# Hybrid attention and RG-LRU layer on one core: projections as three f16 products with ranges found on the chip, instead of three float32r products

## The chip, the cores and the metric

The kernel runs on one NeuronCore of one Trainium2 chip. The metric is device time in microseconds, the median of several executions. For the kernel before it is 510.38 us (three runs, 509.89 to 511.35).

## What is computed

One layer over 1024 tokens with 16 meta tokens ahead of them (T = 1040), model width 1024:

```python
u = rms_norm(h, norm_w, EPS)            # h: meta tokens, then x
proj = u @ w_in                         # 1024 -> 3072
q, k, v, g_att, x_lru, g_lru = split(proj)            # 512 columns each
o = diff_attention(rope(q), rope(k), v, lam, chunk_ids)   # 4 heads, 2 maps each
att_out = rms_norm(o, subln_w) * (1 - lam_init) * silu(g_att)
xc = causal_conv(x_lru, conv_w, width 4) + conv_b
lru_out = rg_lru(xc, w_r, b_r, w_i, b_i, lru_L) * silu(g_lru)
h = h + concat([att_out, lru_out]) @ w_out
out = rms_norm(h, final_norm_w)[16:]
```

All inputs and the output are float32.

## The kernel before

The program is written out in order: each engine carries out its instructions in the order in which the Python code emits them, and nothing reorders them later. A small model of the engines' times (class Clock) only decides where waiting work (lists `bg`, `chains`, `fill`) is emitted between products.

A float32 product is made of three: both operands are split into a hi part and a lo part, and hi*hi, lo*hi and hi*lo are added up in PSUM (`fm_step`, `tm_step`). In the kernel before both parts are float32r. The contraction over 1024 is cut into eight chunks of 128 (k), and the weights come in six groups of 512 columns, in this order:

- **x_lru** (called XL here, L283 to L430). `head_start(k)` loads the k-th chunk of the weights and of x transposed, ScalarE makes the hi part (for x times norm_w), VectorE the lo part, and the products of three of the four channel blocks follow at once, chunk by chunk. The fourth block's products come behind. The row scale 1/rms of each token (`rstd`) is found beside this from a second copy of x (`load_xt`), and is written to DRAM and read back to all partitions (`Rb`); results of the projections are multiplied by it afterwards.
- **k, q, g_att, g_lru** (`run_group`): 32 steps of products each. While one group's products run, the next group's weights are fetched, split by `split_steps` (ScalarE hi, VectorE lo) and kept. Beside k, q and g_att the LRU's convolution, gates (products named psg) and scan are carried out from the list `bg`. k's products take all 1040 tokens in three column pieces (264, 264, 512), the others 512 columns at a time.
- **v, attention and output projection** (`attend`): the score, softmax and weighting steps of eight token tiles, with the products of v and of the output projection (`out_lru`, `out_att`) filled in between. w_out is loaded late by `load_wo`: ScalarE makes the hi part, GpSimd the lo part.

The scales that bring q, k and v into the range of f16 come from the sums of squares of norm_w times the weights (`f16_scale`).

Of the kernel before, what the change touches and what calls it, by code (L numbers as in the profile page):

```python
# [37 lines left out]
class Clock:  # L38
    """Rough times of the engines while the program is written, to place products that can wait
    where TensorE would otherwise stand."""  # L40
# [52 lines left out]
def hybrid_layer_kernel(ctx: ExitStack, tc: tile.TileContext, xT, x, meta, w6, nwT,  # L93
# [56 lines left out]
    def tick(us):  # L150
# [7 lines left out]
        while bg and bg[0][0] <= credit[0]:  # L158
# [4 lines left out]
            if f is None:       # the rest waits for the next chunk of products  # L163
                break
# [10 lines left out]
    CH = 1.25                    # one chunk of six float32r products  # L175

# [1 line left out]
    nw = cst([P, KC], name="nw")  # L178
    nc.gpsimd.dma_start(nw, nwT)
    xs, wt = {}, {}  # L180
    f2 = {g: cst([P, KC], name=f"f2_{g}") for g in (G_Q, G_K, G_V)}
    ss = cst([P, NT + 1], name="ss")
    V.memset(ss, 1.0)
    A.activation(ss, ss, AF.Copy)       # the activation table comes in beside the first loads
# [164 lines left out]
    for t in nxt:  # L349
        load_xt(t)  # L350
# [959 lines left out]
```

## Time and profile before

| | |
|---|---|
| runs | 509.89, 510.38, 511.35 us, median 510.38 |
| profiled execution, first to last instruction | 509.1 us; its whole time isn't listed, the median of the runs is 1.3 us above the span |
| TensorE busy | 473.1 us (93%), 2838 matmuls; weight loads 380.3 us (75%) |
| VectorE busy | 384.1 us (75%), 692 instructions |
| ScalarE busy | 296.8 us (58%), 549 instructions |
| GpSimd busy | 132.7 us (26%), 174 instructions |
| mean granted TensorE clock | 0.976 of full speed |

In the profile's rows PE is TensorE, PEld its weight loads, DVE VectorE, ACT ScalarE, POOL GpSimd, SP the queue that issues most DMAs. A group's row ends with the busy time in us and the mean ns of one instruction, then the idle time of the engine ahead of it. A timeline row has start and length in us, then the instruction, how many were merged, and in brackets the idle time ahead of it with what ended it. A row by windows has the stretch, its length, and the busy time (and number of instructions) of PE, PEld, DVE, ACT and POOL, then the granted clock, the DMA share and GB/s. A busy PE row counts matmuls that overlap one another or wait for weights; so products are measured here by the distance of their starts.

### The profile page before, as it was taken

How to read it: one execution, taken by the hardware profiler on the slowest of the kernel's cores; microseconds unless marked ns; L12 is line 12 of the kernel's file. 1: busy time of each engine (PE TensorE's matmuls, PEld its weight loads, DVE VectorE, ACT ScalarE, POOL GpSimd, SP SyncE). 2: the span in 40 equal slices, each digit the busy share in tenths (PEclk: the TensorE clock that was granted, in tenths of full speed). 3: DMA queues.
4: the chain of work that ended last, by engine and by line, in shares of the span. 5: the costliest groups of instructions: out<-in, count | busy, mean ns of one | idle time of the engine just before them, and what ended most of it. 6: DMA issues, size and time to landing. Idle time of an engine off the chain costs nothing.

```text
span 509.1 us, 7805 instructions
## 1 busy us (share of the span) xinstructions
PE 473.1 (93%) x2838; PEld 380.3 (75%) x2838; DVE 384.1 (75%) x692; ACT 296.8 (58%) x549; POOL 132.7 (26%) x174
## 2 busy tenths in 40 slices
PE   6999939999999999999999999787998899989994
PEld 5998839888888888888876667565776677867774
DVE  5664786693898676974674776899899999999643
ACT  5883532655436838423662466586686776676743
POOL 0110913100110000000100232157142415245772
PEclk9999969999999999999999999999799999989998
DMA  8971801145033114269551126584554374504433
GB/s 255 397 281 41 320 21 38 28 108 163 5 79 82 44 41 166 82 194 304 168 188 37 42 84 169 174 216 145 131 139 121 88 187 125 167 1 163 163 131 124
DMA packets 51366, 68.87 MB, mean 135 GB/s; under 512 B 22096, under 2 KB 31216, under 8 KB 51328
## 3 DMA queue, kind: packets, MB, share of 16 engines
q1 hardware_dynamic: 39456, 55.75, 33.7%
q0 software_dynamic: 11872, 12.63, 10.3%
q8 instruction: 22, 0.36, 0.3%
q14 instruction: 16, 0.13, 0.1%
HBM read 49.44 MB, written 18.91 MB: 134 GB/s over the span
## 4 chain that ended last, share of the span: by engine, by line
PE 56%; DVE 26%; DMA 6%; issue 5%; ACT 4%; POOL 2%; SPq 0%; POOLq 0%; DVEq 0%; ACTq 0%
PE pss L71 34%; DVE e L71 9%; DVE w L71 5%; DVE mx L71 5%; PE psv L71 5%; PE psoa L71 4%; PE psx L71 4%; PE ps L71 3%; PE psg L71 2%; DVE xres L71 2%; DMA r_d<-rstd 1%; PE O L71 1%; DMA Rb<-r_d 1%; DMA idf<-in_ident_dram 1%; ACT sq L71 1%
## 5 line engine op out<-in xcount | busy, mean ns | idle before, releaser
L71 PE MATMUL pss<-xs,w 128*128 128x512 f32 (+1 forms) x720 | 143.5, 347 | 4.7 <-ACT xs L71 4.2
L71 PEld LDWEIGHTS pss<-xs,w 128*128 128x128 f32 x720 | 121.5, 192 | 25.3 <-ACT xs L71 4.2
L71 ACT ACTIVATE e<-e,mx,esc 128x528 f32<-128x528 f32 (+7 forms) x64 | 56.4, 881 | 59.9 <-DVE mx L71 49.6
L71 DVE CUSTOM_DVE_ANT_0 e<-pss,mask 128x528 f32<-128x528 f32 (+7 forms) x64 | 49.0, 766 | 8.9 <-PE pss L71 8.9
L71 DVE TENSOR_TENSOR w<-wraw,w 128x512 fp32r<-128x512 f32 (+2 forms) x49 | 37.4, 780 | 20.6 <-ACT w L71 20.5
L71 PE MATMUL psv<-w,xs 128*128 128x512 f32 x192 | 48.7, 403 | 0.8 <-DVE v L71 0.8
L71 PE MATMUL psol<-woh,lr 128*128 128x512 f32 x128 | 42.7, 414 | 6.1 <-DVE v L71 2.7
L71 PE MATMUL pss<-w,xs 128*128 128x512 f32 x192 | 45.9, 394 | 0.0
L71 PE MATMUL pss<-kst,qt 128*128 128x512 f16 (+3 forms) x208 | 43.8, 324 | 0.6 <-DVE mx L71 0.6
L71 PE MATMUL psoa<-woh,at 128*128 128x512 f32 (+1 forms) x136 | 43.0, 399 | 1.1 <-ACT psoa L71 1.1
L71 PEld LDWEIGHTS psv<-w,xs 128*128 128x128 f32 x192 | 35.3, 188 | 10.6 <-DVE v L71 1.2
L71 PEld LDWEIGHTS pss<-w,xs 128*128 128x128 f32 x192 | 35.7, 188 | 7.9
L71 ACT COPY wT<-pt 128x1024 f16<-128x1024 f16 (+5 forms) x48 | 37.7, 784 | 0.9 <-PE pt L71 0.8
L71 ACT ACTIVATE w<-wraw 128x512 fp32r<-128x512 f32 x47 | 28.5, 619 | 12.8 <-DMA wraw<-in_w_dram 12.3
L71 PE MATMUL ps<-xs,w 128*128 128x512 f32 x120 | 35.0, 400 | 0.0
L71 PEld LDWEIGHTS psol<-woh,lr 128*128 128x128 f32 x128 | 22.9, 188 | 13.5 <-DVE v L71 3.2
L71 PEld LDWEIGHTS <-wT 128*128 128x128 f16 x432 | 27.1, 101 | 7.8 <-issue 5.0
L71 PE MATMUL O<-v,wT 128*128 128x128 f16 x432 | 30.6, 224 | 2.3 <-ACT o L71 2.3
L71 DVE SCALAR_TENSOR_TENSOR e<-e,mx 128x528 f32<-128x528 f32 (+7 forms) x32 | 29.6, 924 | 1.1
L71 POOL COPY wm<-w 128x32 f16<-128x32 f16 x32 | 7.6, 236 | 85.3 <-DVE w L71 84.0
L71 PE MATMUL pt<-idh,w 128*128 128x128 f16 x288 | 25.0, 225 | 5.1 <-ACT wT L71 3.5
L71 PEld LDWEIGHTS psoa<-woh,at 128*128 128x128 f32 x136 | 24.7, 195 | 6.3 <-ACT psoa L71 2.1
(190 smaller groups left out, 874.6 us busy)
## 6 DMA issues: line engine op xcount, KB each, us to landing
wraw<-in_w_dram SPq DMA_DIRECT2D x47, 256.0 KB, 4.2
xt<-in_x_dram SPq DMA_DIRECT2D x8, 512.0 KB, 6.8
woraw<-in_w_out_dram SPq DMA_DIRECT2D x8, 512.0 KB, 4.0
xres<-in_x_dram SPq DMA_DIRECT2D x8, 512.0 KB, 4.5
lr<-lru_d POOLq DMA_DIRECT2D x8, 512.0 KB, 5.1
res_d<-xres SPq DMA_DIRECT2D x8, 512.0 KB, 3.0
res<-res_d SPq DMA_DIRECT2D x8, 512.0 KB, 4.3
out_dram<-res SPq DMA_DIRECT2D x7, 512.0 KB, 2.9
```

The source lines that it names most:

```text
L71: return f(*a, **k)
```

## The change

The hi and lo parts of x, of the projections' weights, of the LRU output and of the attention output, and of w_out, become f16. For their range:

- Each weight group is scaled by the inverse of its whole norm, found on the chip: `square_w` takes squares and their sums on ScalarE, `norm_of` adds them over partitions by a product with ones and takes the power on GpSimd. The split (`split_steps`, now for two chunks of k at a time, 1024 columns) applies the scale. `load_wo` does the same for w_out, and its lo part moves from GpSimd to VectorE.
- x is normed before its split. It is loaded in four pieces of 260 tokens (p = 0 to 3) with all 1024 channels. `square_x` and `sum_x` find the row scales of a piece on the chip: squares on ScalarE, adds on VectorE, small products, a power on GpSimd, a product that spreads the row over all partitions. `split_x` then takes three steps for each of the eight chunks k: VectorE multiplies by norm_w and the row scale, ScalarE casts to hi, VectorE subtracts for lo.
- XL is now done piece by piece: for each p all eight `split_x`, then the products of blocks 0 and 1 (`xl_pair(p, 0)`, 48 products of 260 columns), then those of blocks 2 and 3 in two halves of 24, with `sum_x` of the next piece between the halves. Results are copied out by ScalarE. The weights of the other groups are fetched in two DMAs at the start of a group instead of eight.
- The multiplications by `Rb` and `rstd` after the projections go away, constants take their place, and the LRU output gets a scale per channel (one more pass of squares).

```diff
-    def load_x(k, cuts):
...
-        for c in cuts:
-            hi, lo = xa(0, k, c), xa(1, k, c)
-            A.activation(hi, raw[:, c], AF.Copy, scale=nw[:, k:k + 1])
-            V.scalar_tensor_tensor(lo, raw[:, c], nw[:, k:k + 1], hi.bitcast(F32), op0=OP.mult, op1=OP.subtract)
+    def sum_x(p, s):
+
+        for q in s:
+            V.tensor_tensor(q[:, 0:2], q[:, 0:2], q[:, 2:4], op=OP.add)
+        V.tensor_tensor(s[0][:, 0:2], s[0][:, 0:2], s[1][:, 0:2], op=OP.add)
+        a = s[0]
+        V.tensor_tensor(a[:, 0], a[:, 0], a[:, 1], op=OP.add)
+        ps = bank([XQ, 4], name="psx1")
+        for j in range(4):
+            PE.matmul(ps[:, j:j + 1], a[:, 0, j * XQ:(j + 1) * XQ], ones[:, 0:1], start=True, stop=True)
+        r = const.tile([XQ, 4], F32, tag="rst", bufs=2, name="rst")
+        V.tensor_scalar(r, ps, 2.0 ** -20 / D, EPS * 2.0 ** -20, op0=OP.mult, op1=OP.add)
+        G.tensor_tensor(r, r, pw[0:XQ, 0:4], op=OP.pow)
...
+        PE.matmul(pr_, ones[0:XQ, :], a[0:XQ, 2], start=True, stop=True)
+        return pr_
+
+    def split_x(p, rs, k):
+        s = slice(p * XP, (p + 1) * XP)
+        t = xraw[p, k // 4][:, k % 4]
+        if xs[k] is None:
+            xs[k] = slot("X", [P, 2, T], F16, name="xs")
+        V.scalar_tensor_tensor(t, t, nws[:, k:k + 1], rs, op0=OP.mult, op1=OP.mult)
+        A.activation(xs[k][:, 0, s], t, AF.Copy)
+        V.tensor_tensor(xs[k][:, 1, s], t, xs[k][:, 0, s], op=OP.subtract)
...
+    for p in range(4):
+        ps = two_banks()
+        for c in range(4):
+            if p == 0:
+                split_xl(0, c)
+            for k in (2 * c, 2 * c + 1):
+                split_x(p, rs, k)
+        if p == 0:
+            square_xl(1)
+            lam_steps()
+            for c in range(4):
+                split_xl(1, c)
+        if p < 3:
+            sq = square_x(p + 1)
...
+        xl_pair(p, 0, range(KC), ps)
+        xl_evac(p, 0, ps)
+        ps = two_banks()
+        xl_pair(p, 1, range(4), ps)
+        if p < 3:
+            rs = sum_x(p + 1, sq)
+        xl_pair(p, 1, range(4, KC), ps)
+        xl_evac(p, 1, ps)
+        if p == 1:
+            for h in range(2):
+                square_w(G_K, h)
+            norm_of(G_K, n2w[G_K])
+        if p == 2:
+            for k in range(0, KC, 2):
+                for _ in split_steps(G_K, k):
+                    pass
+            softplus_steps()
+            for h in range(2):
+                conv_scale(h)
...
+        for b, k in enumerate(ks):
+            r, s = raw[b // 2][:, b % 2], v[:, b:b + 1] if j else v[:, 0:1]
+            A.activation(wo[k][:, 0], r, AF.Copy, scale=s)
             yield
+            V.scalar_tensor_tensor(wo[k][:, 1], r, s, wo[k][:, 0], op0=OP.mult, op1=OP.subtract)
             yield
-            G.tensor_tensor(l, r, h.bitcast(F32), op=OP.subtract)
...
-            V.tensor_tensor(r[:, s], r[:, s], ps, op=OP.add)
+            V.scalar_tensor_tensor(r[:, s], ps, woc[0], r[:, s], op0=OP.mult, op1=OP.add)
```

The change's order stands first on ScalarE in the XL stage. Before, hi parts of weights (w) and of x (xs) alternate with squares of x (xt), and each waits for a DMA alone:

```order
L71 ACTIVATE w<-wraw 128x512 [waits DMAHW7_49]
L71 ACTIVATE xs<-xraw,nw 128x528 [waits DMAHW0_49]
L71 ACTIVATE xs<-xraw,nw 128x512 [waits DMAHW1_49]
L71 ACTIVATE xt,ss<-xt 128x1024 [waits DMAHW2_49,Activation_49]
L71 ACTIVATE w<-wraw 128x512 [waits DMAHW3_49]
```

Now, over pieces p = 1 and p = 2, the copies of the products' results (XL) and, ahead of p = 2, the squares of k's weights stand between the hi parts of one piece and of the next:

```order
L71 ACTIVATE xs<-xraw 128x260 [waits DVE_49] x8
L71 ACTIVATE xsq<-xraw 128x1040 [waits DMAHW0_49]
L71 ACTIVATE xsq<-xraw 128x1040 [waits DMAHW1_49]
L71 COPY XL<-pss 128x260 [waits PE_49]
L71 COPY XL<-pss 128x260
L71 COPY XL<-pss 128x260 [waits PE_49]
L71 COPY XL<-pss 128x260
L71 ACTIVATE w,n_3_521<-wraw 128x2048 [waits DMAHW4_49]
L71 ACTIVATE w,n_3_521<-wraw 128x2048 [waits DMAHW5_49]
L71 ACTIVATE xs<-xraw 128x260 [waits DVE_49] x8
```

The hi parts have moved from behind a DMA to behind VectorE's step of the same chunk, and behind the copy of the last products of the piece before.

On VectorE before, each x instruction makes a lo part and waits for its hi part:

```order
L71 SCALAR_TENSOR_TENSOR xs<-xraw,nw,xs 128x528 [waits DMAHW6_49,Activation_49]
L71 SCALAR_TENSOR_TENSOR xs<-xraw,nw,xs 128x512 [waits DMAHW7_49,Activation_49]
L71 TENSOR_TENSOR w<-wraw,w 128x512 [waits DMAHW4_49,Activation_49]
L71 SCALAR_TENSOR_TENSOR xs<-xraw,nw,xs 128x528 [waits DMAHW5_49,Activation_49]
L71 SCALAR_TENSOR_TENSOR xs<-xraw,nw,xs 128x512 [waits DMAHW6_49,Activation_49]
```

Now, in piece p = 0 (wsx is the weights' scale, psx the row scales in PSUM, nws norm_w):

```order
L71 SCALAR_TENSOR_TENSOR w<-wraw,wsx_158,w 128x2x256 [waits DMAHW2_49,Activation_49]
L71 SCALAR_TENSOR_TENSOR xraw<-xraw,nws,psx_149 128x260 [waits DMAHW0_49]
L71 TENSOR_TENSOR xs<-xraw,xs 128x260 [waits Activation_49]
L71 SCALAR_TENSOR_TENSOR xraw<-xraw,nws,psx_149 128x260
L71 TENSOR_TENSOR xs<-xraw,xs 128x260 [waits Activation_49]
L71 SCALAR_TENSOR_TENSOR w<-wraw,wsx_158,w 128x2x256 [waits Activation_49]
```

Each subtraction waits for ScalarE's cast of the product that VectorE wrote directly ahead of it, and the next chunk's multiplication stands behind the subtraction.

On TensorE, the first products wait behind the norm of the second half of the XL weights (n2x_214):

```order
L71 MATMUL psx_149<-xsq,ones 128x260 [waits DVE_49]
L71 MATMUL psf<-n2x_152,ones 128x1 [waits Activation_49]
L71 MATMUL psf<-n2x_214,ones 128x1 [waits PE_49,Activation_49]
L71 LDWEIGHTS w
L71 MATMUL pss<-xs,w 128x260
```

In the kernel before, the first product stands at the head of TensorE's order, with no product ahead of it. The small products of `sum_x` (psx) stand in the same way in the middle of each later pair, as the diff shows.

More of the change, by code (lines that the diff above doesn't have):

```diff
@@ L179, in hybrid_layer_kernel @@
     nc.gpsimd.dma_start(nw, nwT)
[L180 to L184, printed above, removed]
+    idf = cst([P, P], name="idf")
+    nc.gpsimd.dma_start(idf, ident)
+    idh = cst([P, P], F16, name="idh")
+    ones = cst([P, P], name="ones")
+    V.memset(ones, 1.0)
+    pw = cst([P, 16], name="pw")
+    V.memset(pw, -0.5)
+    two = cst([P, 16], name="two")
+    V.memset(two, 2.0)
+    e16 = cst([P, 1], name="e16")
+    V.memset(e16, 2.0 ** -116)
+    mone = cst([P, 1], name="mone")
+    V.memset(mone, -1.0)
+    A.activation(e16, e16, AF.Copy)
+    xs = [None] * KC
+    wt, ws, winv = {}, {}, {}
+    gmax, nws = cst([P, 1], name="gmax"), cst([P, KC], name="nws")
     def half(h):
@@ new lines, in hybrid_layer_kernel, with fetch_w, square_w @@
+    wraw = {}
+    def fetch_w(g, h):
+        r = wraw[g, h] = slot("wr", [P, 4, 512], name="wraw")
+        dma(r, w6[g, h * 512:(h + 1) * 512, :].rearrange("(k p) n -> p k n", p=P))
+    n2w = {}
+    def square_w(g, h):
+        if h == 0:
+            n2w[g] = cst([P, 2], name=f"n2_{g}")
+        j = wtile[g, h] = slot("W", [P, 4, 2, 512], F16, name="w")
+        for k in range(4):
+            wt[g, 4 * h + k] = j[:, k]
+        A.activation(j.rearrange("p k l n -> p (k l n)").bitcast(F32).rearrange("p (k n) -> p k n", k=4),
+                     wraw[g, h], AF.Square, accum_out=n2w[g][:, h:h + 1])
@@ L236, in fm_step, with wpair @@
+    def split_steps(g, k):
+        r = wraw[g, k // 4][:, k % 4:k % 4 + 2]
+        hi, lo = (wpair(g, k, hl) for hl in range(2))
+        A.activation(hi, r, AF.Copy, scale=ws[g])
+        yield 0
+        V.scalar_tensor_tensor(lo, r, ws[g], hi, op0=OP.mult, op1=OP.subtract)
+        yield 1.2
+    wtile = {}
+    def wpair(g, k, hl):
+        return wtile[g, k // 4][:, k % 4:k % 4 + 2, hl, :]
     def fm_step(ps, g, b, k, s):
@@ L613, in qk_evac @@
             V.tensor_tensor(f, f, tmp, op=OP.add)
-        else:
-            for p, pick in parts:
-                V.tensor_tensor(pick(f), p, pick(Rb), op=OP.mult)
-        h = slot("work", [P, n], F16, name="f16h")
-        A.activation(h, f, AF.Copy, scale=sc[:, j:j + 1])
-        yield 1.3
+            parts = ((f, lambda t: t),)
+        for p, pick in parts:
+            A.activation(pick(h), p, AF.Copy, scale=2.0 ** -14)
+        yield 0
         def store(hl, o):
@@ L783, in hybrid_layer_kernel @@
     LK = 1
-    rsv = cst([P, NT + 1], name="rsv")
+    isv = cst([P, 1], name="isv")
     vt = {}
@@ L982, in finish @@
         in_proj.append(i)
-        d["xr"] = slot("work", [P, D], name="res")
+        d["xr"] = slot("X", [P, D], name="res")
         dma(d["xr"], res_d[i])
```

489 lines of the change are left out of this document (237 added, 252 removed).

## The prediction

> **What bounds the kernel now.** I read the page's shares first, then TensorE's timeline at the borders of the stages.
>
> ```profile
> PE 473.1 (93%) x2838; PEld 380.3 (75%) x2838; DVE 384.1 (75%) x692; ACT 296.8 (58%) x549; POOL 132.7 (26%) x174
> PEclk9999969999999999999999999999799999989998
> ```
>
> TensorE is busy almost throughout; the one early dent in the clock is in the slice near 70 us. The borders, by the first product of each stage (XL, k, q, g_att, g_lru, attention):
>
> ```profile
> 4.20 2.00 PE L71 MATMUL pss<-xs,w 128*128 128x264 f32 x6 [4.20 <-ACT xs L71]
> 52.77 0.89 PE L71 MATMUL pss<-xs,w 128*128 128x264 f32 x6
> 113.29 1.54 PE L71 MATMUL pss<-xs,w 128*128 128x512 f32 x6
> 162.18 1.55 PE L71 MATMUL pss<-w,xs 128*128 128x512 f32 x6
> 210.59 44.47 PE L71 MATMUL pss<-xs,w 128*128 128x512 f32 x192
> 254.90 0.64 PE L71 MATMUL pss<-kst,qt 128*128 128x512 f16 x4
> ```
>
> So XL takes 4.2 to 52.8 us with products from 4.2 us on, k to g_lru take 202.1 us, attention 254.2 us. Products bound all but the last stage, where VectorE is as full; this row by windows has VectorE at 18.61 of 20 us:
>
> ```profile
> 330.00:350.00 20.00, 18.71 (x161) 14.14 (x160) 18.61 (x29) 17.62 (x30) 12.46 (x10) 1.00 0.67 168
> ```
>
> **What the f16 products save.** Their price comes from distances between starts, not from busy times.
>
> ```profile
> 85.07 0.90 PE L71 MATMUL pss<-xs,w 128*128 128x264 f32 x6
> 85.81 0.87 PE L71 MATMUL ps<-xs,w 128*128 128x512 f32 x3
> 86.52 0.90 PE L71 MATMUL pss<-xs,w 128*128 128x264 f32 x6
> 300.65 1.04 PE L71 MATMUL pss<-kst,qt 128*128 128x512 f16 x4
> L71 PE MATMUL pss<-xs,w 128*128 128x512 f32 x384 | 90.6, 393 | 0.0
> L71 PE MATMUL pss<-kst,qt 128*128 128x512 f16 x96 | 30.9, 386 | 0.0
> ```
>
> A float32r product of 512 columns: the g_lru stage, (254.90 - 210.59)/192 = 0.231 us. An f16 one: four take 1.04 us, the last lasts 0.386, so three distances are 0.65 us, 0.217 each. That is 14 ns for each product, 2.7 us for a group of 192. A float32r product of 264 columns is 0.74/6 = 0.122 us; f16 by columns 264/512 of 0.217, 0.112 to 0.114. One of k's 32 steps (six of 264, three of 512) so saves 0.09 us, 2.9 us in all. q, g_att and g_lru save 3 x 2.7 = 8.1 us. The gates of the LRU stay float32r.
>
> In k there is a second saving, the wait for the LRU's convolution, which is emitted too early for its data:
>
> ```profile
> 72.17 0.59 PE L71 MATMUL psg<-xch,wgh 128*128 128x264 f32 x1 [7.05 <-ACT xch L71]
> 66.00:68.00 2.00, 0.00 (x0) 0.00 (x0) 2.00 (x3) 0.00 (x0) 0.00 (x0) 0.99 0.00 0
> 68.00:70.00 2.00, 0.00 (x0) 0.00 (x0) 1.93 (x3) 0.00 (x0) 0.00 (x0) 0.50 0.00 0
> 76.00:78.00 2.00, 2.00 (x9) 1.71 (x8) 1.51 (x3) 0.02 (x1) 0.37 (x1) 0.50 0.00 0
> 78.00:80.00 2.00, 2.00 (x12) 1.78 (x12) 1.77 (x4) 0.46 (x1) 0.18 (x1) 0.95 0.00 0
> ```
>
> ```profile
> 58.57 1.25 ACT L71 ACTIVATE xc<-XL,pr 128x1040 f32<-128x1040 f32 x1
> 67.01 3.96 DVE L71 SCALAR_TENSOR_TENSOR xc<-XL,pr,xc 128x1039 f32<-128x1039 f32 x3
> 71.06 1.06 ACT L71 CAST xch<-xc 128x1040 fp32r<-128x1040 f32 x1 [11.24 <-DVE xc L71]
> ```
>
> It costs 7.1 us idle, 0.7 us for the second operand of the gate, some 3.6 us because the products of 72 to 78.5 us run at clock 0.50. In the changed order eight steps of k stand ahead of the first gate (10.6 us), and the chain to it (copies out of PSUM 0.9 and the gate weights 1.0, both by the rows of ScalarE below, then one activation 1.25, three taps 3.96, one cast 1.06) takes about 8 us from the last XL product, so I take this wait as gone: 11.4 us. k to g_lru together: 202.1 - 11.4 - 2.9 - 8.1 = 179.7 us. What is late next there is VectorE's copy-out of q and k, which now holds PSUM until the lo part is made; it has some 10 us of a block's products to do so.
>
> **What the new XL stage costs.** The prices:
>
> ```profile
> L71 DVE SCALAR_TENSOR_TENSOR xs<-xraw,nw,xs 128x264 fp32r<-128x264 f32 x2 | 0.9, 492 | 1.0 <-ACT xs L71 1.0
> L71 ACT ACTIVATE psoa<-res 128x256 f32<-128x256 f32 x2 | 0.8, 376 | 0.7 <-DVE res L71 0.7
> L71 ACT ACTIVATE w<-wraw 128x512 fp32r<-128x512 f32 x47 | 28.5, 619 | 12.8 <-DMA wraw<-in_w_dram 12.3 <-DVE gate L71 0.5
> L71 DVE TENSOR_TENSOR w<-wraw,w 128x128 fp32r<-128x128 f32 x1 | 0.3, 293 | 0.0
> L71 DVE TENSOR_TENSOR w<-wraw,w 128x384 fp32r<-128x384 f32 x1 | 0.6, 559 | 0.0
> L71 ACT ACTIVATE xt<-xt 128x1024 f32<-128x1024 f32 x8 | 8.5, 1062 | 2.5 <-DMA xt<-in_x_dram 2.4
> L71 POOL TENSOR_TENSOR sums<-sums,pw 128x4 f32<-128x4 f32 x8 | 8.8, 1100 | 12.0 <-DVE sums L71 11.5 <-DVE rec L71 0.5
> L71 PE MATMUL psvr<-rsv,sl 16*128 16x1 f32 x2 | 0.4, 256 | 0.0
> L71 POOL TENSOR_TENSOR sc<-f,pw 128x1 f32<-128x1 f32 x3 | 1.7, 559 | 19.7 <-DVE f L71 19.7
> L71 DVE SCALAR_TENSOR_TENSOR f16l<-qk,sc,f16h 128x1024 f16<-128x1024 f32 x4 | 5.1, 1277 | 1.3 <-ACT f16h L71 1.2
> 36.42 0.15 DVE L71 TENSOR_TENSOR nlam<-ld 128x1 f32<-128x1 f32 x1
> 41.88 0.17 DVE L71 TENSOR_SCALAR sp<-sp 128x4 f32<-128x4 f32 x1
> 4.00:5.00 1.00, 0.80 (x2) 0.56 (x3) 0.82 (x2) 0.63 (x3) 0.00 (x0) 1.00 1.00 342
> ```
>
> One chunk of `split_x` is a round trip: VectorE multiplies (0.49), ScalarE casts (about 0.40, between its rows of 256 and 512 columns), VectorE subtracts (0.43, between 128 and 384), with 0.07 for two handovers: 1.39 us, and the next chunk's multiplication stands behind the subtraction. Eight take 11.1 us. Bare sums of the nearest rows bound it at 1.25 and 1.5 us. The 48 products that follow the chunks take 48 x 0.11 = 5.3 us, so TensorE waits for each chunk. And ScalarE's cast for the next piece stands behind the copy of this piece's last products: the round trips don't run beside the pair before.
>
> First product. x's first piece (1.06 MB) lands by 5.9 us at 342 GB/s from about 2.5 us on, the weights behind it. Squares to 7.0; adds (1.8 behind the last square), four small products (0.9, an estimate from psvr's two in 0.4), the power (1.1) and the spreading product to 12.8; norm, scale and first split of the weights to 15.5; four times one weight split (0.75) and two round trips, from 14.8 on, to 28.9; the squares of the weights' second half (2.1, 2048 columns by the 1024-column row) and their norm, behind which TensorE's first product stands: **31 us instead of 4.2**. From there, by stretches:
>
> - p = 0: 48 products, the first 4.5 us at half clock as between 72 and 78 us, 7.5; 24 products 2.6; row scales of p = 1 (small products, 1.1 us of power, VectorE, spreading) 3.3; 24 products 2.6. Ends at 47.0.
> - p = 1: copies and first chunk 1.8, seven round trips 9.7, products of the last chunk 0.7, 24 products 2.6, row scales 3.4 (VectorE's adds end after the squares, which follow the last cast), 24 products 2.6: 20.8. Ends at 67.8.
> - p = 2: as p = 1, and two squares of k's weights with their norm ahead of the first cast, 6.3. Ends at 94.9.
> - p = 3: ahead of the first chunk VectorE has four splits of k's weights (1.28 each behind ScalarE) and the softplus steps (36.42 to 42.05, 5.6 us): first chunk 15.0 us behind the last product; then 9.7 + 0.7 + 5.2. Ends at 125.5.
>
> The half clock after gaps of more than 3 us I put at 3 us more (bounds 0 and the rival below). **k starts at 128.5 us instead of 52.8: 75.7 us later.**
>
> **Attention.** v's 192 products save 2.7 us; of the output products those of the last 35 us, where TensorE is the bound, about 1.2 us. w_out's lo parts become eight VectorE instructions of 1.28 us (10.2 us) and 31 additions become a longer form (0.750 for 0.684, 2.2 us in all). Against that go eight GpSimd passes of 2.4 us, beside which VectorE is slow (the last row has minimum, median and maximum in ns):
>
> ```profile
> L71 POOL TENSOR_TENSOR wol<-woraw,woh 128x1024 fp32r<-128x1024 f32 x8 | 19.7, 2466 | 23.6 <-ACT woh L71 23.6
> L71 DVE TENSOR_TENSOR res<-res,psoa 128x512 f32<-128x512 f32 x15 | 10.3, 684 | 6.5 <-PE psoa L71 6.4
> L71 DVE SCALAR_TENSOR_TENSOR v<-psv,rsv,v 128x512 f16<-128x512 f32 x8 | 5.9, 750 | 11.9 <-ACT v L71 11.9
> L71 DVE SCALAR_TENSOR_TENSOR mx<-mx,nesc,lnsw x64: 219/220/1875, 258.7 to 470.0; 128x1 f32<-128x1 f32 x64
> ```
>
> The one-column instruction takes 0.22 us at the median and up to 1.88; eight stalls of up to 1.6 us are up to 13, of which I take 11. Net +1.5, bounds -1 and +12. Attention: 254.2 - 3.9 + 1.5 = 251.8 us.
>
> **Sum** against the profiled execution: 128.5 + 179.7 + 251.8 = 560.0 us of span. The median of the runs lies 1.3 us above that span, so 561 us.
>
> **Rivals.**
>
> *TensorE stays at half clock in XL (581 us).* The clock fell to 0.50 between 66 and 70 us, some 3 us after the last product, and came back only at 78.5 us, after 4.5 us of dense products. In XL TensorE will work about half of the time. At 0.217 us for a product of 260 columns a chunk's six take 1.3 us, just hidden in 1.39; the second pairs would cost 5.2 us more in each piece and the tails of the first 0.6: 5.2 + 3 x 5.8 = 22.6, less the 3 counted. Against it: at half clock the chunks keep TensorE busy 94% of the time, which should bring the clock back. [...]
>
> *Round trips overlap (546 us).* If VectorE's subtraction cost only what its pipeline adds, a chunk is 0.9 us, 15 us less over 32 chunks. The order speaks against it.
>
> *Splits run ahead of the products (506 us, faster).* If the chunks of piece p + 1 were made while piece p's products run, XL would be bound by its 384 products of 0.11 us, 42 us from 31 us on, and k would start at 73 us: 55.5 us less. It would no longer be slower as soon as XL ended before 77.7 us, since k to the end gains 24.8. For it: VectorE needs only about 7 us of instructions for a piece. Against it: ScalarE's copy ahead of the casts waits for the piece's last product.
>
> *VectorE pays for w_out (572 us)*: the stalls beside GpSimd stay, and the 10.2 us come on top. It is the bound on Attention.
>
> *The f16 products are no cheaper (576 us)*: f16 weights and columns then run at 0.231, and the 2.9 + 8.1 + 3.9 us are not saved; the row of scores speaks against it.
>
> **How the numbers follow.** Forecast 65%, half clock 14%, VectorE's w_out 8%, overlap 5%, no cheaper products 3%, splits ahead 5%. The likeliest case gives 561 us. Its own range is 551 to 572: round trips at the bounds of 1.25 and 1.5 us are -4 and +4 over 32, the row scales and DMAs +-4, the stages after it +-5. The range of 8 in 10 reaches to the overlap with its spread and to the half clock: 541 to 583. A measurement can tell about 0.3% from no change; of splits ahead 4 in 5 would come out faster and the rest as no change, so faster 4%, no change 1%, slower 95%.
>
> **What would show it.** The first XL product near 31 us; TensorE's rows of XL in four clumps with waits of 0.7 us for VectorE's xs between chunks, and waits of 8 us and 16 us ahead of the third and fourth; k's first product near 128 us; no wait of 7 us for xch; the distance of products of 512 columns at 0.217 us; g_lru's stage at 42 us. If chunks of xs for the next piece show beside products of the piece before, or k starts before 80 us, the prediction is wrong.

## The result: 580.95 us, and the profile after

The changed kernel takes 580.95 us (median of four runs, 579.57 to 583.77) against 510.13 of the kernel before (508.93 to 511.35 beside it): a ratio of 1.140, interval 1.136 to 1.144. The profiled execution took 579.57 us, its span is 577.8. The shares on its page, to be set beside those of before:

```profile
PE 470.5 (81%) x2987; PEld 271.0 (47%) x2987; DVE 388.2 (67%) x763; ACT 320.3 (55%) x550; POOL 110.2 (19%) x180
PE   1166666299999999979999988976799889889884
```

By its busy time TensorE did no more work than before (470.5 us against 473.1), and it stood still for 71 us more (span less busy time). The second line is its busy share in 40 slices: the first eight, up to 115 us, are at one to six tenths. TensorE's timeline after, at the first product of XL, at the clumps that follow waits, and at the borders of the stages k, q, g_att, g_lru and attention:

```profile
34.70 10.04 PE L71 MATMUL pss<-xs,w 128*128 128x260 f16 x72
47.49 2.82 PE L71 MATMUL pss<-xs,w 128*128 128x260 f16 x24
77.61 2.80 PE L71 MATMUL pss<-xs,w 128*128 128x260 f16 x11 [2.10 <-ACT xs L71]
111.95 6.83 PE L71 MATMUL pss<-xs,w 128*128 128x260 f16 x31 [13.72 <-ACT xs L71]
128.14 0.81 PE L71 MATMUL ps<-xs,w 128*128 128x512 f16 x3
174.41 1.47 PE L71 MATMUL pss<-xs,w 128*128 128x512 f16 x6
221.94 7.93 PE L71 MATMUL pss<-w,xs 128*128 128x512 f16 x36
272.57 19.59 PE L71 MATMUL pss<-xs,w 128*128 128x512 f16 x90
314.14 0.63 PE L71 MATMUL pss<-kst,qt 128*128 128x512 f16 x4
```

The row of 128.14 is k's first product of 512 columns; six products of 264 stand 0.66 us ahead of it (the distance of the later such pairs), so k starts at 127.5. All starts of k below are read this way. So XL ends 74.7 us later than before, k to g_lru take 186.7 us instead of 202.1, and attention 263.7 instead of 254.2. What TensorE waited for (total us, times, longest):

```profile
PE psf L71 <- ACT w L71: 21.7, 2, 17.1
PE pss L71 <- ACT xs L71: 16.9, 3, 13.7
PE psx L71 <- DVE xsq L71: 11.2, 5, 3.7
PE psf L71 <- ACT wo L71: 8.7, 2, 4.7
PE psn L71 <- DMA idf<-in_ident_dram: 7.8, 1, 7.8
PE pss L71 <- DVE gsig L71: 4.3, 1, 4.3
```

The first three and the fifth are in XL: the norms of weights, the first cast of a piece, the row scales, and the load ahead of the range of norm_w. They are 57.6 us. Within a piece the waits hide in the distance of chunks. VectorE and ScalarE in one chunk of p = 0 and at the start of the next:

```profile
30.07 0.48 DVE L71 SCALAR_TENSOR_TENSOR xraw<-xraw,nws,psx 128x260 f32<-128x260 f32 x1
31.04 0.43 DVE L71 TENSOR_TENSOR xs<-xraw,xs 128x260 f16<-128x260 f32 x1 [0.49 <-ACT xs L71]
31.38 0.48 DVE L71 SCALAR_TENSOR_TENSOR xraw<-xraw,nws,psx 128x260 f32<-128x260 f32 x1
30.58 0.42 ACT L71 ACTIVATE xs<-xraw 128x260 f16<-128x260 f32 x1 [1.21 <-DVE xraw L71]
```

From multiplication to multiplication it is 1.31 us, of which VectorE waits 0.49 for the cast.

### The profile page after: what moved, and what is told of

It is laid out like the page before. It is cut to its first block, busy times and chain, and to the rows that moved or that the text cites. A ratio compares the mean times of both kernels' runs of the same rounds, so it can differ in the third digit from the quotient of the medians.

```text
span 577.8 us, 7981 instructions
## 1 busy us (share of the span) xinstructions
PE 470.5 (81%) x2987; PEld 271.0 (47%) x2987; DVE 388.2 (67%) x763; ACT 320.3 (55%) x550; POOL 110.2 (19%) x180
## 4 chain that ended last, share of the span: by engine, by line
DVE 36%; PE 35%; ACT 16%; issue 8%; POOL 3%; DMA 1%; POOLq 0%; ACTq 0%; DVEq 0%
PE pss L71 22%; DVE e L71 9%; DVE w L71 5%; DVE mx L71 4%; PE ps L71 4%; PE psv L71 3%; DVE a L71 2%; ACT w L71 2%; ACT xs L71 2%; DVE xraw L71 2%; DVE gate L71 2%; ACT wo L71 2%; DVE xs L71 2%; ACT e L71 2%; PE psg L71 1%
## 5 line engine op out<-in xcount | busy, mean ns | idle before, releaser
L71 PE MATMUL pss<-xs,w 128*128 128x260 f16 (+2 forms) x960 | 168.4, 328 | 23.0 <-ACT xs L71 16.9
L71 PEld LDWEIGHTS <-w 128*128 128x128 f16 x1344 | 125.6, 101 | 109.8 <-issue 39.7
L71 PEld LDWEIGHTS <-xs 128*128 128x128 f16 x384 | 37.2, 100 | 51.4 <-issue 10.6
L71 DVE CUSTOM_DVE_ANT_0 e<-pss,mask 128x528 f32<-128x528 f32 (+7 forms) x64 | 49.0, 765 | 12.1 <-PE pss L71 11.9
L71 PE MATMUL psol<-wo,lr 128*128 128x512 f16 x192 | 47.0, 392 | 5.4 <-DVE v L71 3.5
L71 PE MATMUL psoa<-wo,at 128*128 128x512 f16 (+1 forms) x204 | 46.5, 376 | 4.8 <-POOL at L71 2.8
L71 PE MATMUL pss<-w,xs 128*128 128x512 f16 x192 | 44.6, 389 | 4.3 <-DVE gsig L71 4.3
L71 PE MATMUL psv<-w,xs 128*128 128x512 f16 x192 | 45.1, 387 | 0.1
L71 PEld LDWEIGHTS <-at 128*128 128x128 f16 x204 | 20.0, 100 | 25.3 <-issue 5.0
L71 DVE SCALAR_TENSOR_TENSOR w<-wraw,ws,w 128x1024 f16<-128x1024 f32 x20 | 24.9, 1260 | 6.9 <-ACT w L71 6.9
L71 ACT ACTIVATE gate<-psg,pr 128x264 f32<-128x264 f32 (+1 forms) x24 | 12.9, 548 | 28.7 <-PE psg L71 28.7
L71 DVE RECIPROCAL a<-a 128x208 f32<-128x208 f32 x20 | 27.6, 1418 | 0.0
## 6 DMA issues: line engine op xcount, KB each, us to landing
kst<-k_d SPq DMA_DIRECT2D x4, 520.0 KB, 10.2
```

The source lines that it names most:

```text
L71: return f(*a, **k)
```

## The experiments

Twelve kernels, one profiled run each. They are best read by stage: no edit of XL changed the length of attention by more than 0.3 us, and the edits of attention left k to g_lru at 186.7 us. The edits are shown in short; a comment or three dots stand for lines left out. Start of k, length of k to g_lru, length of attention and span, in us:

| kernel | k starts | k to g_lru | attention | span |
|---|---|---|---|---|
| changed kernel | 127.5 | 186.7 | 263.7 | 577.8 |
| 1 next chunk first | 117.3 | 186.7 | 263.7 | 567.7 |
| 2 second norm early | 126.8 | 186.7 | 263.9 | 577.4 |
| 3 k's weights behind | 113.0 | 195.1 | 263.8 | 571.9 |
| 4 products that keep TensorE busy | 130.8 | 186.7 | 263.9 | 581.4 |
| 5 splits ahead | 81.6 | 194.2 | 263.6 | 539.4 |
| 6 as 5, lo parts of x on GpSimd | 81.5 | 195.0 | 263.6 | 540.1 |
| 7 as 5, constant for w_out, early adds | 81.6 | 195.4 | 257.3 | 534.3 |
| 8 as 7, TensorE kept busy | 79.1 | 194.7 | 257.1 | 530.9 |
| 9 w_out's squares spread | 130.2 | 186.7 | 263.3 | 580.2 |
| 10 constant for w_out | 127.5 | 186.7 | 257.4 | 571.6 |
| 11 lo parts of w_out on GpSimd | 127.6 | 186.7 | 266.7 | 581.0 |
| 12 as 10, lo parts of w_out on ScalarE | 131.4 | 186.7 | 251.0 | 569.1 |

Kernels 9 to 12 have the changed kernel's XL code, yet their k starts between 127.5 and 131.4; experiment 4 shows where the difference comes from. A difference of under 4 us in XL is no effect by itself. The expectations of experiments 4 to 8 read k's start from its second step (128.8 us in the changed kernel, 82.9 in kernel 5), which is 1.3 us later than in the table.

### 1. Is the chunk a round trip?

```diff
 V.scalar_tensor_tensor(t, t, nws[:, k:k + 1], rs, ...)          # chunk k
 A.activation(xs[k][:, 0, s], t, AF.Copy)
-V.tensor_tensor(xs[k][:, 1, s], t, xs[k][:, 0, s], op=OP.subtract)
+# the subtraction of chunk k is emitted behind the multiplication of chunk k + 1
```

> Starting point is the changed kernel: span 577.8 us, first XL product at 34.7, k's first product at 127.5, attention 263.7 us long. Here the multiplication of the next chunk of x stands on VectorE ahead of the subtraction of this chunk; the subtraction then finds its hi part made. Theory round trip: a chunk takes VectorE's two instructions alone, 0.48 + 0.43 = 0.91 us instead of 1.31, so 0.40 us less for each of 32 chunks, 12.8 us at the most; k's first product at 115 to 118, time 567 to 570 us. Rival half clock: six products of a chunk at half speed take 6 x 0.217 = 1.30 us, so the chunks of p = 1 to 3 stay at 1.3 us and only the chunks of p = 0, ahead of which no product stands, gain: 3 us, time 577 us.

569.5 us; k starts 10.2 us earlier. VectorE's rows of p = 1, and TensorE's from its first product to the row scales:

```profile
49.46 0.48 DVE L71 SCALAR_TENSOR_TENSOR xraw<-xraw,nws,psx 128x260 f32<-128x260 f32 x1
49.85 0.42 DVE L71 TENSOR_TENSOR xs<-xraw,xs 128x260 f16<-128x260 f32 x1
50.19 0.48 DVE L71 SCALAR_TENSOR_TENSOR xraw<-xraw,nws,psx 128x260 f32<-128x260 f32 x1
49.13 0.27 PE L71 MATMUL pss<-xs,w 128*128 128x260 f16 x1 [1.06 <-ACT xs L71]
58.07 0.60 PE L71 MATMUL psx<-ones,xsq 128*65 128x1 f32 x8
```

VectorE waits no more, and a chunk takes 0.73 us instead of 1.31: less than the 0.91 that I had added up from busy times, since one instruction's row begins before the last one's ends. The 72 products take 8.9 us instead of 13.1 (51.38 to 64.50 in the changed kernel). With 0.58 less in 32 chunks, 18.6 us could have come; 10.2 did. Of the other 8.4, 3.1 went to half clock in the last products of p = 1 (24 take 5.40 us instead of 2.83; from the row of 58.07 to the first product of p = 2 it is 16.2 us, 13.1 in the changed kernel; experiment 4 has the clock beside such rows), 2.4 stayed in p = 0, where splits of the weights that wait for ScalarE stand between the chunks, and 2.9 in p = 1 to 3, the last two of which are slower (the first 38 products of p = 2 take 5.50 us, 0.87 for six; the 102 of p = 3 take 12.9, where 16.2 less eight times 0.58 would be 11.6). The round trip is shown, and half clock was not the bound.

### 2. What does the late first product cost?

```diff
     square_xl(0)
+    square_xl(1)          # was behind the splits of p = 0
```

> Starting point is the changed kernel (first XL product 34.7 us, its 96 products of p = 0 done at 50.3, span 577.8). Here the squares and the norm of the second half of the XL weights stand directly behind those of the first half, ahead of the splits of p = 0. Theory handover: TensorE's first product is no longer held, it comes at about 21 us and the first 48 products of p = 0 run beside its splits; but the splits start 2.1 us later (ScalarE's squares), and what ends p = 0 is VectorE's chain of row scales of p = 1 (last split, weight splits 2.7, adds 2.5, products, power): p = 0 ends at 47 instead of 50.3, time 577 us. Rival: the late first product is the cost itself, its 14 us come back in full, p = 0 ends at 37 to 38 and the time is 566 us.

579.2 us. TensorE's rows: the first product, the last 24 of p = 0, and the last 24 of p = 1.

```profile
20.24 3.01 PE L71 MATMUL pss<-xs,w 128*128 128x260 f16 x12 [3.07 <-ACT xs L71]
42.07 4.49 PE L71 MATMUL pss<-xs,w 128*128 128x260 f16 x24
64.29 5.40 PE L71 MATMUL pss<-xs,w 128*128 128x260 f16 x24
```

The handover theory holds. The first product came 14.5 us earlier, but the last 24 products of p = 0 could begin only 5.4 us earlier (42.07 against 47.49), as the row scales of p = 1 allow. Then the clock (a mean of 0.942 in this execution, 0.956 in the changed kernel's) took gain back: these products took 4.49 us (2.82 in the changed kernel), so p = 0 ended at 46.6 instead of 50.3, and those of p = 1 took 5.40 (2.83). k starts 0.7 us earlier. The second loss, 3.1 us with the small products ahead of it, comes and goes without any edit (experiment 4). So the wait of 17.1 us, the largest row of the list above, was worth 3.8 us where that loss is left out, and 0.7 in this execution.

### 3. Do k's weights in the queues make the two long waits?

```diff
-        if p == 1:     # squares of k's weights, norm
-        if p == 2:     # splits of k's weights, softplus steps, conv_scale
+        if p == 2:     # squares behind square_x(3); norm behind xl_pair(2, 1)
+        if p == 3:     # splits, softplus steps, conv_scale behind the split_x of p = 3
```

> Starting point is the changed kernel (waits of TensorE ahead of the pieces p = 2 and p = 3 of 7.2 and 13.7 us, k's first product 127.5, span 577.8). Here the squares of k's weights stand on ScalarE behind the casts of p = 2 and their norm behind that piece's products; the splits of k's weights, the softplus steps and the scales of the convolution stand on VectorE behind the splits of p = 3. Theory queue: both waits shrink to the 1.5 to 2 us that the wait ahead of p = 1 and its first chunk take; 5.5 + 12 us less, k's first product at 109 to 111. Behind it the convolution now starts up to 5 us later against k's products, since VectorE's 10.7 us of moved work hides only 6 us beside the last products of p = 3; a wait for xch of 2 to 4 us may come back. Time 562 to 566 us. Rival bound of work: VectorE's work moves with it and delays k's copies by as much: time 575 us or more.

573.67 us. TensorE's waits ahead of p = 2 and p = 3, and one row each of q and g_att:

```profile
72.02 0.27 PE L71 MATMUL pss<-xs,w 128*128 128x260 f16 x1 [1.06 <-ACT xs L71]
96.29 0.27 PE L71 MATMUL pss<-xs,w 128*128 128x260 f16 x1 [2.11 <-ACT xs L71]
197.60 2.72 PE L71 MATMUL pss<-xs,w 128*128 128x512 f16 x6 [4.86 <-DVE f16l L71]
237.96 0.59 PE L71 MATMUL psf<-n,ones 128*128 128x2 f32 x2 [4.01 <-ACT w L71]
```

The queue theory holds for XL: the waits of 4.5 + 2.1 and 13.7 us are now 1.1 and 2.1, and k starts 14.5 us earlier, at 113.0. That is 2 us later than expected: the last 24 products of p = 2 ran at half clock (5.35 us from 88.71 us on). And k to g_lru take 8.4 us longer: not by a wait for xch, as I expected, but by a wait for a copy-out in q and one for the squares of the next group's weights in g_att, each followed by half clock (0.83 over the 20 us around it). So the time lies above the theory's range. These two waits come 85 us and more behind the moved work, whose order on VectorE is not touched there; why they fall there was not tried further.

### 4. What does half clock cost in XL?

```diff
+    def warm(n, s):      # n products that nothing reads, into a bank of their own
+            warm(38, ...); norm_of(G_K, n2w[G_K]); warm(14, ...)     # behind p = 1
+            warm(118, ...)                                           # behind p = 2
```

> Starting point is the changed kernel itself (waits of 4.5 and 2.1 us ahead of p = 2, of 13.7 us ahead of p = 3, clock 0.50 behind them; k's first product 128.8 us, span 577.8). Here 170 products that nothing reads are put into these waits (38 and 14 ahead of p = 2, 118 ahead of p = 3). Theory of the forecast: the half clock costs XL about 3 us, since the chunks of p = 2 and p = 3 follow one another at 1.31 us at either clock and only the last products of each piece are slower; k starts at 125 to 127 us, span 574 to 576. Rival half clock: it is the bound of these pieces, and full clock brings 5 us or more for each of them: k at 118 us or earlier, span 567 or less.

583.17 us, k 3.3 us later: against both theories, by a third thing. TensorE's rows of the two kernels for the last 24 products of p = 1, ahead of which their programs are the same; first the changed kernel:

```profile
67.06 0.68 PE L71 MATMUL psx<-xsq,ones 65*128 65x260 f32 x2 [1.95 <-DVE xsq L71]
67.57 2.83 PE L71 MATMUL pss<-xs,w 128*128 128x260 f16 x24
```

and the kernel with the added products, and the first product of its p = 2 with the row scales behind its chunks:

```profile
67.44 1.20 PE L71 MATMUL psx<-xsq,ones 65*128 65x260 f32 x2 [1.96 <-DVE xsq L71]
68.43 5.39 PE L71 MATMUL pss<-xs,w 128*128 128x260 f16 x24
80.84 0.27 PE L71 MATMUL pss<-xs,w 128*128 128x260 f16 x1 [0.53 <-ACT xs L71]
96.53 0.68 PE L71 MATMUL psx<-xsq,ones 65*128 65x260 f32 x2 [1.95 <-DVE xsq L71]
```

Windows over the wait and the products behind it, in which the granted clock is the number behind the five busy times, in the changed kernel and then in this one:

```profile
65.00:66.00 1.00, 0.10 (x2) 0.02 (x1) 0.16 (x1) 0.00 (x0) 0.55 (x1) 1.00 0.00 0
66.00:67.00 1.00, 0.00 (x0) 0.00 (x0) 0.43 (x1) 0.00 (x0) 0.45 (x1) 1.00 0.00 0
67.00:68.00 1.00, 0.94 (x6) 0.78 (x7) 0.00 (x0) 0.00 (x0) 0.00 (x0) 1.00 0.00 0
68.00:69.00 1.00, 1.00 (x11) 0.88 (x10) 0.00 (x0) 0.00 (x0) 0.00 (x0) 1.00 0.08 16
```

```profile
65.00:66.00 1.00, 0.48 (x8) 0.39 (x7) 0.16 (x1) 0.00 (x0) 0.18 (x1) 1.00 0.00 0
66.00:67.00 1.00, 0.00 (x0) 0.00 (x0) 0.14 (x1) 0.00 (x0) 0.83 (x1) 0.93 0.00 0
67.00:68.00 1.00, 0.56 (x2) 0.50 (x3) 0.29 (x1) 0.00 (x0) 0.00 (x0) 0.50 0.00 0
68.00:69.00 1.00, 1.00 (x5) 0.59 (x4) 0.00 (x0) 0.00 (x0) 0.00 (x0) 0.50 0.09 16
```

Behind the same wait (1.95 and 1.96 us) the granted clock was 0.50 in one execution, up to 73 us, and 1.00 in the other. Half clock cost 2.6 us in the 24 products and 0.5 in the small ones ahead of them. It isn't the chip: kernels 1, 2, 3 and 9 ran on one chip, and these 24 products took 5.40, 5.40, 2.83 and 4.49 us there. What decides between the two was not shown.

What the experiment was made for it shows too: p = 2 took 15.7 us from its first product to the row scales (80.84 to 96.53) with its waits filled, and 15.6 in the changed kernel (77.61 to 93.19), whose first 5.4 us were at half (0.50 over 77.6 to 83.0 us); p = 3 took 16.2 up to k's row in both, though in the changed kernel its first 5.2 us were at half (0.51 over 112.0 to 117.2). The first 31 products of p = 2 in the changed kernel, at 0.50 up to 83.0 us, take 7.02 us (77.61 to 84.63), which is 0.46 for the first and 1.31 for each of five chunks; at 1.00 the chunks behind them are 1.31 apart too (84.63, 85.94, 87.25). Half clock behind a long wait cost these chunks nothing, since six products at 0.217 us (24 took 5.20 us in this kernel, from 68.43 to the next row at 73.63) hide in 1.31.

### 5. Splits ahead of the products

```diff
+    for p in range(4):      # split_x(0 ..) and the row scales of p = 1 stand ahead of the loop
+        g = sum_x(square_x(p + 2))            # adds, small products and spread as steps of their own
+        split_x(p + 1, rs, k) for k in 0 .. 3
+        xl_pair(p, 0, ...)
+        split_x(p + 1, rs, k) for k in 4 .. 7; xl_evac(p, 0, ps)
+        xl_pair(p, 1, ...); rs = next(g); xl_evac(p, 1, ps)
```

> Starting point is the changed kernel (k's first product 128.8 us, span 577.8). Here the splits of piece p + 1 stand ahead of the copies of piece p's products on ScalarE and run beside them, the row scales are made two pieces ahead with their small products between the pairs, the multiplication of the next chunk stands ahead of this chunk's subtraction, the norm of the second half of the XL weights is made early, and k's weights follow behind the last piece. Theory order (XL is long because its steps wait for one another, not because of their work): VectorE's work for XL is 32 chunks of 0.91 (29), four row scales of 2.9 (12), weight splits 6 and k's weights 5, from about 15 us on; XL ends and k starts at 74 to 84 us; behind it q and g_att lose up to 10 us, as where k's weights alone were moved; time 530 to 545 us. Rival work: TensorE's 384 products at half clock (83 us from 21 us on) or VectorE's chunks at 1.31 keep k's start above 100 us; time 555 us or more.

541.21 us, as expected. XL by windows (stretch, length, busy time of PE, PEld, DVE, ACT, POOL, then the clock):

```profile
30.00:40.00 10.00, 3.46 (x21) 2.26 (x20) 7.98 (x14) 6.80 (x10) 1.47 (x1) 0.70 0.54 205
50.00:60.00 10.00, 10.00 (x96) 8.85 (x94) 8.99 (x22) 4.94 (x13) 1.00 (x1) 1.00 0.01 2
```

From 42 us on TensorE runs without a gap: 45.9 of the 74.7 us that XL had lost were order, not work. k to g_lru lose 7.5 us, by the same two waits as in experiment 3 (4.8 us in q, 4.0 in g_att), so 38.4 us are left in the span.

### 6 to 8. Three additions to it

Kernel 6 has `G.tensor_tensor` for the subtraction of `split_x`; kernel 7 has the constant of experiment 10 and calls `norm_range()` behind the first adds; kernel 8 adds 58 products that nothing reads to kernel 7, in the waits of 29.8 to 38 us.

> Starting point is the kernel with splits ahead (k's first product 82.9 us, span 539.4). Here the subtraction that makes the lo part of x is GpSimd's instead of VectorE's; everything else stands as there. Theory VectorE: from 20 to 45 us TensorE still waits for chunks of VectorE's 0.91 us; with 0.48 on VectorE and the subtraction (about 0.63 us, from the 2.47 us of 1024 columns) beside it on GpSimd a chunk takes 0.65, the eight chunks of p = 1 gain 2 us, those of p = 0 3, and VectorE is ahead when k starts, so q loses less: k at 77 to 80, span 528 to 535. Rival neighbours: VectorE is slower beside GpSimd and the longer round trip (multiply, cast, subtract on three engines) delays the last chunk of each piece: k at 83 or later, span 539 or more.

541.92 us: no difference. The 13.5 us that left VectorE were not what TensorE waited for; between 30 and 42 us it waits for the chain of the next row scales (6.7 us in three waits for xsq).

> Starting point is the kernel with splits ahead (span 539.4). Here the scale of w_out is the constant as well (its squares, sums and norm are left out), and the instructions that find the range of norm_w stand behind the adds of the first row scale on VectorE and TensorE, so that these adds no longer wait until 10.2 us. Theory sum: the parts add up: 6.3 us from the constant in attention, 2 to 2.7 us from the earlier adds, k's first product at 80 to 81 us, span 530 to 532. Rival: the first adds wait for the squares instead, which come behind x's DMA, and gain under 1 us; the gain of the constant depends on where the products of v stand and is met again as another wait: span 535 to 540.

536.06 us. The constant brought its 6.3 us in attention. The early adds brought the first product from 20.7 to 19.0 and k not at all, and k to g_lru took 1.2 us longer; the span of 534.3 lies between the two ranges. The 48 products behind the gap, in kernel 7 and then kernel 8:

```profile
39.95 8.36 PE L71 MATMUL pss<-xs,w 128*128 128x260 f16 x48
48.14 0.60 PE L71 MATMUL psx<-xsq,ones 65*128 65x260 f32 x2
```

```profile
39.42 5.48 PE L71 MATMUL pss<-xs,w 128*128 128x260 f16 x48
45.65 0.68 PE L71 MATMUL psx<-xsq,ones 65*128 65x260 f32 x2 [0.75 <-DVE xsq L71]
```

> Starting point is the kernel with splits ahead, a constant for w_out and the early adds (first XL product 19.0 us, the 48 products of p = 0 that start at 39.95 take 8.4 us at a granted clock of 0.50 to 45.9, k's first product 82.9, span 534.3). Here 58 products that nothing reads are put into TensorE's waits between 29.6 and 39.9 us (22 ahead of the first small products of the row scales, 26 behind them, 10 behind the product that spreads them), into a bank of their own. Theory clock: TensorE is halved because it idles there; kept busy it stays at full speed, the 48 products take 5.3 us, k starts at 79.5 to 80.5 us, span 531 to 532. Rival: what ends the pair is VectorE's weight splits and the next row scales, the clock hides only a wait; k stays at 82 to 83, or starts later by the added products.

532.69 us, as the theory of the clock said; k starts 2.5 us earlier, at 79.1: kept busy, TensorE did the 48 products in 5.48 us, and a further 0.75 us wait then showed. The granted clock was 0.50 from 38 to 44 us in kernel 7; over the whole span it is 0.958 there and 0.971 in kernel 8. Here the clock does cost, because the products stand close behind the gap (8.36 us for the 48 in kernel 7), and it had eaten the gain of the early adds. This is the fastest form of the change that I found, 4.7% above the kernel before on the same chip (508.62 us), and it leaves out the range of w_out, for which the constant stands.

### 9. Do the waits for w_out's squares cost attention their length?

```diff
-            if b % 2:
-                yield
+            yield
+            yield                       # one square per two steps
+        for _ in range(4):
+            yield
         norm_of(f"o{j}", n2)
```

> Starting point is the changed kernel (attention 263.7 us, in it two waits of TensorE of 3.9 and 4.7 us for the squares of w_out ahead of the product psf that adds them up). Here the eight passes of squares are made one per two steps of the schedule instead of two per step, and the norm is made four steps behind the last of them. Theory order: the product psf finds its sums ready, the two waits go, attention takes 254 to 257 us, time 570 to 573 us. Rival VectorE: attention is bound by VectorE, whose work with w_out's lo parts is the same; the waits of TensorE go but are met again as waits for VectorE, and the time stays at 577 to 580 us.

581.99 us, attention 263.3, as the rival said; the time is above its range because k started 2.7 us later by the clock (the last 24 products of p = 0 and of p = 1 took 4.34 and 4.49 us, 2.82 and 2.83 in the changed kernel). The waits of 8.7 us are gone, and others are there instead, of which two are:

```profile
382.95 1.86 PE L71 MATMUL pss<-kst,qt 128*128 128x512 f16 x4 [2.71 <-DVE mx L71]
410.61 1.11 PE L71 MATMUL pa<-idf,o 128*128 128x128 f32 x4 [5.46 <-POOL o L71]
```

My reading of the list of waits, that these two waits were the excess of attention, fell here. The kernel also made the second set of squares in one stretch still, so it didn't fully do what was meant.

### 10 to 12. What of w_out costs attention?

Kernel 10 leaves the squares, their sums and the norm out, kernel 11 makes the lo parts on GpSimd, kernel 12 is kernel 10 with the lo parts written by ScalarE.

```diff
-        ... A.activation(..., AF.Square, scale=by[b], accum_out=n2[:, b:b + 1]); norm_of(f"o{j}", n2)
+        V.memset(ws[f"o{j}"], 2.0 ** 9); V.memset(winv[f"o{j}"], 2.0 ** -9)                 # 10, 12
-            V.scalar_tensor_tensor(wo[k][:, 1], r, s, wo[k][:, 0], op0=OP.mult, op1=OP.subtract)
+            G.tensor_tensor(wo[k][:, 1], r, wo[k][:, 0], op=OP.subtract)                    # 11
+            A.activation(wo[k][:, 1], r, AF.Copy, scale=s)                                  # 12
```

> Starting point is the changed kernel, whose attention stage takes 263.7 us against a forecast of 251.8. Here the norm of w_out is left out: its scale is a constant set by a memset, so the eight passes of squares on ScalarE (1.13 + 0.19 us each), the two products psf, and the chain to the scale go; hi and lo parts of w_out are made as in the changed kernel. Theory norm chain: TensorE and VectorE stand still for the two norms (8.7 and 7.8 us), and these and ScalarE's 10.6 us are the excess: attention 252 to 256 us, time 569 to 573 us. Rival lo parts: VectorE's eight passes of 1.3 us for w_out's lo parts are the excess, the norm is not: attention 260 to 264 us, time 577 to 580.

573.35 us, attention 257.4: 6.3 us are the norm's. Above the theory's 252 to 256, below the rival's 260.

> Starting point is the changed kernel, attention stage 263.7 us. Here w_out's lo parts are made on GpSimd as in the kernel before (raw minus hi, without the scale, so the lo parts hold other numbers); the norm stays. Theory norm chain: the excess of 12 us lies in the norm, VectorE loses 10.7 us of passes and gets back up to that in slower instructions beside GpSimd: attention 258 to 264 us. Rival lo parts: VectorE is the bound from the first passes on, attention shrinks by the passes' 10 us to 253 to 256 us, time 567 to 571.

582.78 us, attention 266.7, above both ranges. GpSimd's passes, and VectorE's one-column instructions in the kernel before, in the changed kernel and in this one (busy time, mean ns):

```profile
L71 POOL TENSOR_TENSOR wo<-woraw,wo 128x1024 f16<-128x1024 f32 x8 | 17.5, 2189 | 12.9 <-ACT wo L71 12.9
```

```profile
L71 DVE SCALAR_TENSOR_TENSOR mx<-mx,nesc,lnsw 128x1 f32<-128x1 f32 x64 | 23.0, 359 | 2.3
```

```profile
L71 DVE SCALAR_TENSOR_TENSOR mx<-mx,nesc,lnsw 128x1 f32<-128x1 f32 x64 | 18.4, 287 | 2.3
```

```profile
L71 DVE SCALAR_TENSOR_TENSOR mx<-mx,nesc,lnsw 128x1 f32<-128x1 f32 x64 | 25.7, 402 | 2.3
```

64 instructions of one column cost VectorE 7.3 us more beside GpSimd, most of the 10.7 us that it was spared; its busy time in the whole stage fell only from 201.0 to 200.3 us. Why the stage got 3.0 us longer isn't shown.

> Starting point is the kernel with a constant scale for w_out (attention 257.4 us, of the changed kernel's 263.7; the forecast had 251.8). Here w_out's lo parts are copied by ScalarE (the hi values again, so the lo parts hold other numbers) and VectorE's eight passes of 1.28 to 1.34 us are left out; ScalarE has room for them, since its squares are left out as well. Theory VectorE: VectorE is the bound of the stage and these passes are what stands between 257.4 and the forecast; attention takes 248 to 252 us, time 563 to 567 us. Rival idle: in the stretch where the passes fall VectorE also waits for other engines, the passes fill such waits, and attention stays at 255 to 258 us, time 571 to 574 us; what is missing is then the 3.9 us by which the f16 products were to shorten the stage, which VectorE's later full stretch doesn't let through.

570.84 us; attention 251.0, in the theory's range. The time is above that range because k started 3.9 us later by the clock (the last 24 products of p = 1 took 5.41 us, 2.83 in the changed kernel). VectorE's lo parts, 10.2 us of passes in kernel 10, cost attention 6.4 us.

## Why the prediction was right, and where it was wrong

The forecast's time was 561, the result 580.95, inside the range of 541 to 583 but 20 us above the likeliest case and outside that case's own range. By terms:

- **XL: right by its mechanism; that it was right to 1 us is in part luck.** k was to start at 128.5 and started at 127.5. The round trip, put at 1.39, is 1.31 (shown by experiment 1); its bounds of 1.25 and 1.5 don't follow from its rows, whose bare sums are 1.16 and 1.67. The waits of 8 and 16 us ahead of the third and fourth clump are 7.2 (70.4 to 77.6) and 13.7, and come from k's weights in the queues (experiment 3). The four pieces took 15.6, 20.1, 27.8 and 29.3 us where the sum had 16.0, 20.8, 27.1 and 30.6. Misses cancelled: the first product came 3.7 us late, 2.9 of them already at the product that spreads the row scales (15.7 instead of 12.8); 1.7 of these are the first adds, which stood behind the range of norm_w and its load that ends at 7.8 us (experiment 7). Against that, the 3 us for half clock, a term that no run shows, were only 1.7, all in p = 2 (granted clock 0.50 over 93.2 to 96.6 us; 4.01 us for its last 24 products instead of 2.83, and 0.5 in the small ones ahead of them), and the other pieces came 2.4 us short.
- **The rival of half clock throughout (581 us) gave the time that came, by a mechanism that did not.** TensorE's products ran at half clock only over the first 5.4 us of p = 2 and 5.2 us of p = 3 (0.50 and 0.51) and in the last products of p = 2, and with the waits filled their chunks stayed as they were (experiment 4). A time that fits is no proof.
- **f16 products: right.** g_lru's 192 products take 41.57 us, 0.2165 each, and the wait for xch is gone: k takes 46.9 us, 46.2 by the terms. The half clock behind that wait had been put at 3.6 us; by the prediction's own rows it is 3.0 (half the time from 72.2 to 78.2 us).
- **k to g_lru: 186.7 instead of 179.7, the first wrong step.** k is 0.7 us over its terms, q 1.3, g_att 4.9, g_lru nothing. The prediction named VectorE's copy-out of q and k as late next and gave it "some 10 us of a block's products to do so". In q that wasn't enough: 1.4 us of wait for f16l. The larger wait, 4.3 us in g_att, is for another copy-out (gsig), which had no term, with half clock behind it (0.91 over 20 us). VectorE's step for gsig stood behind four reciprocals and the next weights' norm:

```profile
256.66 2.74 DVE L71 RECIPROCAL a<-a 128x208 f32<-128x208 f32 x2
259.32 1.16 DVE L71 SCALAR_TENSOR_TENSOR gsig<-pss,gsig 128x1024 f32<-128x1024 f32 x1
260.53 12.17 PE L71 MATMUL pss<-w,xs 128*128 128x512 f16 x48 [4.26 <-DVE gsig L71]
```

Why they came so late can be read one step further back. VectorE's wait for ScalarE's gate ahead of these steps, in the kernel before and then in the changed kernel:

```profile
195.30 1.24 DVE L71 SCALAR_TENSOR_TENSOR gate<-gate,a 128x1040 f32<-128x1040 f32 x1 [4.37 <-ACT gate L71]
```

```profile
248.02 1.24 DVE L71 SCALAR_TENSOR_TENSOR gate<-gate,a 128x1040 f32<-128x1040 f32 x1 [8.50 <-ACT gate L71]
238.53 1.91 ACT L71 ACTIVATE w<-wraw 128x2048 f32<-128x2048 f32 x1
```

ScalarE now makes the squares of the next group's weights in the middle of the gate's steps, two passes of about 2.1 us each with the read of their sums (the second at 241.35). They are the size of the 4.1 us by which VectorE's wait grew, and the prediction's sum for k to g_lru has no term for norms. No run takes them out, so this cause is read from the rows and not shown.

- **Attention: 263.7 instead of 251.8, the second wrong step.** The sum had w_out's lo parts and the longer additions, and no price for its squares and norm, which the change adds as plainly: 6.3 us (experiment 10). The lo parts were booked at -0.8 (10.2 us of passes less 11 us of stalls); they cost 6.4 against ScalarE's copies, and 3.0 less than on GpSimd. The term of 11 us was too large: the 64 one-column instructions that it was read from went from 23.0 to 18.4 us, 4.6 less, and the only other large group of one column, 32 instructions, from 12.1 to 9.7. Without norm and lo parts, attention takes 251.0, about the forecast's number, but not by its terms: without the lo parts these would give 241.5 (254.2 - 3.9 + 2.2 - 11). About 4 of the 9.5 us between are, by these rows, stalls that were not there to be saved; the rest stays open. VectorE has 190 us of work in this stage of kernel 12 and had 204 in the kernel before, so its work alone doesn't explain it. (The longer additions, put at 2.2 us, are 2.0 by their rows, 31 x 0.066.)
- **Splits ahead, 506 us by the rival.** The reordered kernel gave 541: XL 8.6 us longer than its 73, 7.5 in k to g_lru, and the two wrong steps above.

## What to carry to other kernels

When a split needs a result of another engine in the middle, emit the next piece's first step ahead of this piece's last, and keep the preparation of the next group's weights out of the queues between two pieces: here that order was worth 46 us in XL and 38 in the whole span, the cheaper products of k to g_lru 11 by the forecast's terms. A wait's length in a list of waits is not its price: removing 17.1 us brought 3.8 at the most, removing 8.7 us nothing, while eight passes of VectorE for which TensorE's list had no row were worth 6.4. Price every instruction that the change adds, the norms too, by the stage in which it stands.

## What the runs showed of the hardware

- **Behind one and the same wait the granted clock was once 0.50 and once 1.00.** A wait of 1.95 us, with eight one-column products (0.6 us) ahead of it, was followed by 0.50 in kernel 4 and by 1.00 in the changed kernel, and the 24 products behind it took 5.39 and 2.83 us (experiment 4). k's start moved by up to 3.9 us between kernels with the same XL code (127.5 to 131.4); the four runs of the changed kernel spread over 4.2 us, 579.57 and 579.67 us at a mean clock of 0.956, 583.77 and 582.23 at 0.951 and 0.950.
- **Work at half speed was free in one place, and a shorter wait was worth nothing in another.** The chunks of p = 2 in the changed kernel were 1.31 us apart at 0.50 and at 1.00 (experiment 4). In kernel 7 the products began 1.6 us earlier than in kernel 5 (39.95 and 41.53 us) and ended at the same time (48.2): the full clock came back at 45.9 us in kernel 7 and at 44.3 in kernel 5. In kernel 7 5.9 us of products ran at half clock behind the gap.
- **Rows of VectorE overlap.** Two instructions of 0.48 and 0.42 us follow one another every 0.73 us when neither waits (experiment 1); the sum of busy times, 0.90, overstates such a chain by nearly a quarter.
